# Two transformer blocks in float32: the last column block of the final matmul in three token parts, with accumulating stores

## The chip, the core and the metric

The kernel runs on one core of a Trainium2 chip. A core has five engines that each run their own instructions in order: TensorE (matmuls; PE in the profile, and PEld for its weight loads), VectorE (DVE), ScalarE (ACT), GpSimd (POOL) and SyncE (SP, which here only issues transfers). Transfers can also be issued from ScalarE's and GpSimd's queues. The metric is the time of one execution on the device in microseconds.

## The reference, cut to what matters

Two blocks run one after the other on x, 512 tokens by 1024 channels, in float32. The first holds two gated feed-forward layers and two kinds of attention; the second a convolution, a recurrent mixer and a feed-forward layer with a short convolution. The change touches only the end of the second block:

```python
z = causal_dwconv(h @ w_up, ffn_dw_w, ffn_dw_b)
z_gate, z_val = jnp.split(z, 2, axis=-1)
f = (jax.nn.silu(z_gate) * z_val) @ w_down        # (512, 2816) @ (2816, 1024)
x = x + gt_f * rms_norm(f, ffn_post_g)            # the mean of squares runs over 1024 channels
```

The root mean square of f needs all 1024 channels of a token before any channel of that token can be scaled and added to x.

## The kernel before

Everything is kept transposed: channels lie on the 128 partitions, tokens along the columns, so a tile is 128 channels by 512 tokens and x has eight of them. Each float32 matmul is made of three float32r matmuls (`mm3`, L358): weights and data are split into a high and a low part, and high times high, high times low and low times high are summed in one PSUM bank. The weights come from memory on SyncE's queue, ScalarE rounds the high part and VectorE subtracts to get the low one (`split_weights`, L347). Sums that need no split, such as the mean of squares, are plain fp32 matmuls, which the trace shows as two passes each.

The last stage is `conv_ffn` (L1563). The up matmul gives 22 pairs `hs` of hidden tiles (names hh and hl). Then come eight column blocks m of the down matmul. For m = 0 to 6 a block is 22 × 3 matmuls of 512 tokens (`dense_steps`, L369); its result is squared into `acc` and copied with its gain to `fs[m]` (`done`, L1603). The last block, m = 7, is done in two halves of 256 tokens by `dense_halves` (L420): all 66 matmuls of the first half, then all 66 of the second, from weight tiles that stay in SBUF. `finish(h)` (L1610) sums acc and the last block's squares over the partitions with two matmuls against a constant 1/1024 (`rstd`, L486), forms the reciprocal root in `nrsqrt` (L495; three ScalarE and two VectorE steps), multiplies each of the eight `fs` tiles by it, adds the product to x and stores it in turn through SyncE's and ScalarE's queue. `finish(0)` is issued after the third k of the second half, `finish(1)` after the last matmul.

The program is written in this order, and a scheduler then places the instructions on each engine by their dependences; buffers are taken from pools whose reuse adds waits. Each engine runs its list strictly in that order, so an issue of a transfer that waits holds back all that stands behind it on its engine.

Of the kernel before, what the change touches and what calls it, by code (L numbers as in the profile page):

```python
# [15 lines left out]
ALU = mybir.AluOpType  # L16
# [3 lines left out]
P = 128  # L20
T = 512
D = 1024
KD = D // P
# [2 lines left out]
NH = 8  # L26
BIG = 1.0e30
HALF = slice(0, T // 2), slice(T // 2, T)

# [208 lines left out]
def weave(*streams):  # L240

    total = [sum(c for c, _ in s) or 1.0 for s in streams]
    done, at = [0.0] * len(streams), [0] * len(streams)
    while True:
        left = [i for i, s in enumerate(streams) if at[i] < len(s)]
        if not left:
            return
        i = min(left, key=lambda i: (done[i] + 0.5 * streams[i][at[i]][0]) / total[i])
        cost, f = streams[i][at[i]]
        at[i] += 1  # L250
        done[i] += cost
        f()
# [3 lines left out]
class Net:  # L256
# [160 lines left out]

        return [(1.9, parts), (0.9, sums)]

    def dense_halves(self, src, x, last, done, mid):  # L420

        nk, ws = len(x), []
        for k in range(0, nk, 8):
            n = min(8, nk - k) * P
            part = src[:, k * P : k * P + n]
            ws.append(self.weights(part, n) if k < 16 else self.weights_at(part, n, last))
        for h in range(2):
            ps = self.bank()[:, : T // 2]
            for k in range(nk):
                s = slice(k % 8 * P, k % 8 * P + P)  # L430
                self.mm3(ps, [w[:, s] for w in ws[k // 8]], [t[:, HALF[h]] for t in x[k]], k == 0, k == nk - 1)
                if h == 1:
                    for f in mid.pop(k, ()):
                        f()
            done(h, ps)

    def group_halves(self, src, n, x, room, side, ws=(), done=None, W=6):
# [101 lines left out]
    def swiglu(self, acc, gname, gu, down, new2=None, side=(), start=None):  # L539


        nc = self.nc
        new = self.acc()
        side = list(side)
        with self.phase("h", False) as ph:
            self.log_exp()
            r = self.tmp("r", 1)
            hs = []

            def hidden(pg, pu):  # L550
                m = len(hs)
                s = self.tmp("s")
                nc.vector.tensor_mul(s, pg, r)  # L553
                nc.scalar.activation(s, s, AF.Silu, scale=-1.0)
                self.anchor = nc.vector.tensor_mul(s, s, pu).ins  # L555
                hi = ph.tile([P, T], F32R, tag=f"hh{m}", name=f"hh{m}_{self.n}")
                lo = ph.tile([P, T], F32R, tag=f"hl{m}", name=f"hl{m}_{self.n}")
                self.halves(hi, lo, s)
                hs.append((hi, lo))

            if start is not None:
                self.warm()
                xs = []

                def arrive(k):
                    xs.append(self.first(k))
                    return xs[k]

                ps = self.group(start, 6, arrive)
                self.rstd(self.sq0, self.c("mean"), r)  # L570
                for m in range(3):
                    hidden(ps[2 * m], ps[2 * m + 1])
            else:
                xs = [self.gained(k, self.v(gname, k)) for k in range(KD)]
            for m in range(len(hs), MF):
                pg, pu = self.bank(), self.bank()
                at = gu.shape[0] - 2 * (MF - m)
                self.dense(pg, gu[at], xs)
                if m == 0:
                    self.rstd(acc, self.c("mean"), r)  # L580
                self.dense(pu, gu[at + 1], xs)
                hidden(pg, pu)
                for f in side[:1]:
                    side.pop(0)()
            nc.vector.tensor_scalar_mul(r, r, -0.5)

            def done(m, ps, c=slice(0, T)):
                x = self.x[m][:, c]
                t = self.tmp("s")[:, c]
                nc.vector.tensor_mul(t, ps, r[:, c])  # L590
                self.anchor = nc.vector.tensor_add(x, x, t).ins
                self.add_square(new[:, c], x, m == 0)
                if new2 is not None:
                    self.add_square(new2[:, c], x, m == 0, self.v("fin_g", m))
                    nc.gpsimd.dma_start(self.dY[m][:, c], x)

            if new2 is not None:
                self.entry(new, new2)
            last = KD if new2 is None else KD - 1
            for m in range(last):  # L600
                ps = self.bank()
                n = -(-len(side) // (last - m))
                weave(self.dense_steps(lambda: ps, down[m], hs, split=4), [(1.3, f) for f in side[:n]])
                side = side[n:]
                done(m, ps)
            if new2 is not None:
                enter = [lambda k=k: self.enter(0, k) for k in (None, *range(KD))]
                mid = {4: enter[:1], 5: enter[1:7], 13: enter[7:]}
                tiles = [ph.tile([P, D], F32R, tag="ada", name=f"ada_{self._n()}", bufs=2) for _ in range(2)]
                self.log_exp()  # L610
                self.dense_halves(down[KD - 1], hs, tiles, lambda h, ps: done(KD - 1, ps, HALF[h]), mid)
        return new

    def entry(self, acc1, acc2):
# [948 lines left out]
    def conv_ffn(self, xs, first):  # L1563
        nc, A = self.nc, self.A
        ngt = self.columns(KD)
        nc.vector.scalar_tensor_tensor(ngt, self.mod[:, 40:48], -1.0, self.v("fpost"), op0=ALU.mult, op1=ALU.mult)
        with self.phase("h2", False) as ph:
            tile_ = lambda shape, tag, dt=F32, bufs=1: ph.tile(list(shape), dt, tag=tag, name=f"{tag}_{self._n()}", bufs=bufs)
            hs, zs = {}, {}
# [33 lines left out]
            def done(m, ps, c=slice(0, T)):  # L1603
                if m < KD - 1:
                    self.add_square(acc[:, c], ps, m == 0)
                else:
                    nc.scalar.activation(sq[:, c], ps, AF.Square)
                nc.scalar.activation(fs[m][:, c], ps, AF.Copy, scale=ngt[:, m : m + 1])

            def finish(h):  # L1610
                c = HALF[h]
                self.rstd(acc[:, c], self.c("mean"), r[:, c], last=sq[:, c])
                for k in range(KD):
                    f, x = fs[k][:, c], self.x[k][:, c]
                    nc.vector.tensor_mul(f, f, r[:, c])  # L1615
                    nc.vector.tensor_add(x, x, f)  # L1616
                    (nc.sync if k % 2 == 0 else nc.scalar).dma_start(self.out[k * P : (k + 1) * P, c], x)

            for m in range(KD - 1):
                weave(self.dense_steps(self.bank, A["down2"][m], hs, lambda ps: done(m, ps)))  # L1620
            tiles = [tile_([P, D], f"w{n}", F32R) for n in ("hi", "lo")]
            self.log_exp()
            self.dense_halves(
                A["down2"][KD - 1], hs, tiles, lambda h, ps: done(KD - 1, ps, HALF[h]), {2: [lambda: finish(0)]}
            )
            finish(1)

    def _n(self):
        self.n += 1
# [40 lines left out]
```

## Time and profile before

| | |
|---|---|
| time, median of 3 runs | 1696.13 us (1695.34 to 1698.58) |
| the profiled execution | 1687.92 us, span 1686.1 us |
| TensorE busy | 1649.4 us (98%) |
| its weight loads busy | 1337.2 us (79%) |
| VectorE, ScalarE, GpSimd busy | 1022.9, 716.9 and 51.3 us |
| TensorE's share of the chain that ended last | 89% |
| bytes moved, mean rate | 177.15 MB, 105 GB/s |

A busy TensorE is not one at its peak: matmuls overlap, and a matmul's duration in the profile holds the time that its last column needs to come out. The step from one start to the next is what a stream of them costs. The chain that ended last is followed back from the last instruction; the other engines' time counts only where they are on it.

### The profile page before, as it was taken

To read this page: it belongs to the slowest core of one execution; us is meant where nothing else is said; L and a number is where in the kernel's file an instruction comes from. 1 tells how busy PE (TensorE), PEld (TensorE's weight loads), DVE (VectorE), ACT (ScalarE), POOL (GpSimd) and SP (SyncE) were. 2 spreads that over 40 slices of the span, in tenths; PEclk is the share of its full clock that TensorE was granted. 3 is DMA by queue.
4 is the path that set the end of the run, shared out by engine and by line. 5 is a ranking of instruction groups with operands and counts; after the bars stand their busy time and mean duration, and the time that the engine had idled before them with its cause. 6 is when DMAs were issued, how large, how long until landed. Compare 5 with 4: busy or idle time off the path is not lost.

```text
span 1686.1 us, 21795 instructions
## 1 busy us (share of the span) xinstructions
PE 1649.4 (98%) x8596; PEld 1337.2 (79%) x8596; DVE 1022.9 (61%) x1706; ACT 716.9 (43%) x1167; POOL 51.3 (3%) x104
## 2 busy tenths in 40 slices
PE   9999999999999999999999999998989999999997
PEld 7888888876776788888888887786768988888886
DVE  4555545546888564555334469998777676665224
ACT  4432232237679553223222354633357454444222
POOL 0000000000000000000000010000000000000000
PEclk9999999999999999999999999998999999999999
DMA  5344445534111234443333332221042123333332
GB/s 204 117 146 143 140 126 195 176 100 131 51 62 32 69 90 147 150 149 116 97 100 112 118 114 65 95 71 40 19 141 70 61 87 100 96 92 96 100 95 85
DMA packets 63862, 177.15 MB, mean 105 GB/s; under 512 B 17065, under 2 KB 19369, under 8 KB 63760
## 3 DMA queue, kind: packets, MB, share of 16 engines
q1 hardware_dynamic: 52016, 138.96, 26.5%
q0 software_dynamic: 9872, 34.71, 6.5%
q10 hardware_dynamic: 1872, 2.10, 0.4%
q8 instruction: 67, 1.10, 0.3%
q14 instruction: 35, 0.29, 0.1%
HBM read 169.19 MB, written 6.55 MB: 104 GB/s over the span
## 4 chain that ended last, share of the span: by engine, by line
PE 89%; DVE 6%; ACT 2%; DMA 1%; issue 0%; ACTq 0%; SPq 0%; DVEq 0%
PE ps L321 88%; PE ps L869 1%; DVE Ts L1166 1%; DVE Tm L1163 0%; DMA raw<-in_w_out 0%; DVE acc L484 0%; DVE wlo L351 0%; DVE f L1615 0%; DVE x L1521 0%; DVE x L992 0%; DVE x L1616 0%; DVE x L1522 0%; DMA raw<-in_w_in2k 0%; DMA x<-in_x 0%; DMA dpm<-dY 0%
## 5 line engine op out<-in xcount | busy, mean ns | idle before, releaser
L350 ACT CAST whi<-raw 128x1024 fp32r<-128x1024 f32 (+1 forms) x244 | 249.0, 1021 | 628.1 <-PE ps L321 580.4
L351 DVE TENSOR_TENSOR wlo<-raw,whi 128x1024 fp32r<-128x1024 f32 (+1 forms) x244 | 288.9, 1184 | 256.2 <-ACT whi L350 250.2
L321 PE MATMUL ps<-xh,whi 128*128 128x512 f32 (+1 forms) x1008 | 400.9, 399 | 1.2 <-ACT xh L514 1.2
L321 PE MATMUL ps<-xh,wlo 128*128 128x512 f32 (+1 forms) x1008 | 391.3, 389 | 1.5 <-DVE wlo L351 1.4
L321 PE MATMUL ps<-xl,whi 128*128 128x512 f32 (+1 forms) x1008 | 391.4, 388 | 0.3 <-DVE xl L515 0.3
L321 PEld LDWEIGHTS ps<-xh,whi 128*128 128x128 f32 x1008 | 189.8, 188 | 51.3 <-issue 5.8
L321 PEld LDWEIGHTS ps<-xl,whi 128*128 128x128 f32 x1008 | 189.8, 188 | 44.2 <-issue 5.3
L321 PEld LDWEIGHTS ps<-xh,wlo 128*128 128x128 f32 x1008 | 189.2, 188 | 41.9 <-DVE wlo L351 2.2
L321 PE MATMUL ps<-hh,whi 128*128 128x512 f32 (+1 forms) x560 | 210.5, 376 | 0.0
L321 PE MATMUL ps<-hh,wlo 128*128 128x512 f32 (+1 forms) x560 | 209.8, 375 | 0.0
L321 PE MATMUL ps<-hl,whi 128*128 128x512 f32 (+1 forms) x560 | 209.8, 375 | 0.0
L321 PE MATMUL ps<-oh,whi 128*128 128x512 f32 (+1 forms) x360 | 134.8, 375 | 0.0
L321 PE MATMUL ps<-ol,whi 128*128 128x512 f32 (+1 forms) x360 | 134.5, 374 | 0.0
L321 PE MATMUL ps<-oh,wlo 128*128 128x512 f32 (+1 forms) x360 | 134.2, 373 | 0.0
L321 PEld LDWEIGHTS ps<-hh,whi 128*128 128x128 f32 x560 | 105.4, 188 | 19.9 <-issue 0.8
L321 PEld LDWEIGHTS ps<-hl,whi 128*128 128x128 f32 x560 | 105.4, 188 | 18.9
L321 PEld LDWEIGHTS ps<-hh,wlo 128*128 128x128 f32 x560 | 105.4, 188 | 18.8
L555 DVE TENSOR_TENSOR s<-s,ps 128x512 f32<-128x512 f32 x44 | 30.1, 687 | 133.0 <-PE ps L321 133.0
L321 PEld LDWEIGHTS ps<-ol,whi 128*128 128x128 f32 x360 | 68.2, 189 | 12.2 <-issue 0.2
L321 PEld LDWEIGHTS ps<-oh,whi 128*128 128x128 f32 x360 | 68.0, 189 | 12.0 <-issue 0.2
L321 PEld LDWEIGHTS ps<-oh,wlo 128*128 128x128 f32 x360 | 68.0, 189 | 11.9
L553 DVE TENSOR_TENSOR s<-ps,r 128x512 f32<-128x512 f32 x44 | 30.2, 691 | 73.6 <-PE ps L321 73.5
(444 smaller groups left out, 2173.5 us busy)
## 6 DMA issues: line engine op xcount, KB each, us to landing
raw<-in_ffn_gu SPq DMA_DIRECT2D x82, 512.0 KB, 3.7
ada<-in_ada_w POOLq DMA_DIRECT2D x48, 512.0 KB, 3.9
raw<-in_up SPq DMA_DIRECT2D x38, 512.0 KB, 3.6
raw<-in_ffn_d SPq DMA_DIRECT2D x32, 512.0 KB, 3.7
raw<-in_w_in SPq DMA_DIRECT2D x27, 512.0 KB, 3.6
raw<-in_w_out SPq DMA_DIRECT2D x16, 512.0 KB, 3.6
raw<-in_down SPq DMA_DIRECT2D x16, 512.0 KB, 3.6
raw<-in_ffn_d SPq DMA_DIRECT2D x16, 384.0 KB, 3.2
```

Source lines behind the costliest of these rows:

```text
L321: self.nc.tensor.matmul(*a, **k)
L350: nc.scalar.copy(hi[:, :n], raw[:, :n])
L351: nc.vector.tensor_sub(lo[:, :n], raw[:, :n], hi[:, :n].bitcast(F32))
L553: nc.vector.tensor_mul(s, pg, r)
L555: self.anchor = nc.vector.tensor_mul(s, s, pu).ins
L869: nc.tensor.transpose(ps[:, i * P : (i + 1) * P], es[u, i][:, j * P : (j + 1) * P], self.c("ident"))
L1166: ins = nc.vector.tensor_add(t[:, i + 1 :, :c], t[:, i + 1 :, :c], o)
```

## The change

The last block's 512 tokens are cut in three parts, 256, 128 and 128 (`LAST`); `dense_halves` becomes `dense_parts`, which takes the parts and a table `mid` of work by part and k. The sum for the root is split: `begin(h)` issues the matmul of acc before a part's end (after k = 18 of the same part), `finish(h)` the matmul of the squares, after k = 4 of part 1 for part 0, after k = 6 of part 2 for part 1, and at the end for part 2. The four even x tiles are stored to the output as they are, in the code after m = 3; their products are then added to the output in memory by accumulating transfers from GpSimd. The four odd tiles are added on VectorE as before, into the product's tile, and stored through SyncE and ScalarE. The other user of the function, the first block's end, keeps its two halves.

```diff
--- before.py
+++ after.py
@@ -26,6 +26,7 @@
 NH = 8
 BIG = 1.0e30
 HALF = slice(0, T // 2), slice(T // 2, T)
+LAST = slice(0, T // 2), slice(T // 2, T // 4 * 3), slice(T // 4 * 3, T)
 
 
 
@@ -417,21 +418,20 @@
 
         return [(1.9, parts), (0.9, sums)]
 
-    def dense_halves(self, src, x, last, done, mid):
+    def dense_parts(self, src, x, last, done, mid, parts=HALF):
 
         nk, ws = len(x), []
         for k in range(0, nk, 8):
             n = min(8, nk - k) * P
             part = src[:, k * P : k * P + n]
             ws.append(self.weights(part, n) if k < 16 else self.weights_at(part, n, last))
-        for h in range(2):
-            ps = self.bank()[:, : T // 2]
+        for h, c in enumerate(parts):
+            ps = self.bank()[:, : c.stop - c.start]
             for k in range(nk):
                 s = slice(k % 8 * P, k % 8 * P + P)
-                self.mm3(ps, [w[:, s] for w in ws[k // 8]], [t[:, HALF[h]] for t in x[k]], k == 0, k == nk - 1)
-                if h == 1:
-                    for f in mid.pop(k, ()):
-                        f()
+                self.mm3(ps, [w[:, s] for w in ws[k // 8]], [t[:, c] for t in x[k]], k == 0, k == nk - 1)
+                for f in mid.pop((h, k), ()):
+                    f()
             done(h, ps)
 
     def group_halves(self, src, n, x, room, side, ws=(), done=None, W=6):
@@ -605,10 +605,10 @@
                 done(m, ps)
             if new2 is not None:
                 enter = [lambda k=k: self.enter(0, k) for k in (None, *range(KD))]
-                mid = {4: enter[:1], 5: enter[1:7], 13: enter[7:]}
+                mid = {(1, 4): enter[:1], (1, 5): enter[1:7], (1, 13): enter[7:]}
                 tiles = [ph.tile([P, D], F32R, tag="ada", name=f"ada_{self._n()}", bufs=2) for _ in range(2)]
                 self.log_exp()
-                self.dense_halves(down[KD - 1], hs, tiles, lambda h, ps: done(KD - 1, ps, HALF[h]), mid)
+                self.dense_parts(down[KD - 1], hs, tiles, lambda h, ps: done(KD - 1, ps, HALF[h]), mid)
         return new
 
     def entry(self, acc1, acc2):
@@ -1607,23 +1607,39 @@
                     nc.scalar.activation(sq[:, c], ps, AF.Square)
                 nc.scalar.activation(fs[m][:, c], ps, AF.Copy, scale=ngt[:, m : m + 1])
 
+            def begin(h):
+
+                c = LAST[h]
+                st[h] = ps = self.bank()[:, : c.stop - c.start]
+                self.mm(ps, self.c("mean"), acc[:, c], start=True, stop=False)
+
             def finish(h):
-                c = HALF[h]
-                self.rstd(acc[:, c], self.c("mean"), r[:, c], last=sq[:, c])
-                for k in range(KD):
-                    f, x = fs[k][:, c], self.x[k][:, c]
+
+                c, ps = LAST[h], st[h]
+                self.mm(ps, self.c("mean"), sq[:, c], start=False, stop=True)
+                self.nrsqrt(r[:, c], ps, acc[:, c], 1e-6)
+                for k in (0, 2, 4, 6, 1, 3, 5, 7):
+                    f, o = fs[k][:, c], self.out[k * P : (k + 1) * P, c]
                     nc.vector.tensor_mul(f, f, r[:, c])
-                    nc.vector.tensor_add(x, x, f)
-                    (nc.sync if k % 2 == 0 else nc.scalar).dma_start(self.out[k * P : (k + 1) * P, c], x)
-
+                    if k % 2 == 0:
+                        nc.gpsimd.dma_start(o, f, accum_op=ALU.add)
+                    else:
+                        nc.vector.tensor_add(f, f, self.x[k][:, c])
+                        (nc.sync if k % 4 == 1 else nc.scalar).dma_start(o, f)
+
+            st = {}
             for m in range(KD - 1):
                 weave(self.dense_steps(self.bank, A["down2"][m], hs, lambda ps: done(m, ps)))
+                if m == 3:
+                    for k in range(0, KD, 2):
+                        nc.sync.dma_start(self.out[k * P : (k + 1) * P, :], self.x[k])
             tiles = [tile_([P, D], f"w{n}", F32R) for n in ("hi", "lo")]
             self.log_exp()
-            self.dense_halves(
-                A["down2"][KD - 1], hs, tiles, lambda h, ps: done(KD - 1, ps, HALF[h]), {2: [lambda: finish(0)]}
-            )
-            finish(1)
+            work = lambda f, h: [lambda: f(h)]
+            mid = {(0, 18): work(begin, 0), (1, 4): work(finish, 0), (1, 18): work(begin, 1), (2, 6): work(finish, 1)}
+            mid[2, 18] = work(begin, 2)
+            self.dense_parts(A["down2"][KD - 1], hs, tiles, lambda h, ps: done(KD - 1, ps, LAST[h]), mid, LAST)
+            finish(2)
 
     def _n(self):
         self.n += 1
```

TensorE at the program's end. `ps_…` is the bank that is written, `hh`, `hl` the data, `whi`, `wlo` the weights, `acc` and `sq` the squares, `cst` the constants; the last column is partitions by columns. Before:

```order
L321 MATMUL ps_13197<-hh_1592_12397,whi_13109 128x256
L321 MATMUL ps_13197<-hl_1593_12398,whi_13109 128x256
L321 MATMUL ps_13197<-hh_1592_12397,wlo_13110 128x256
L321 MATMUL ps_13197<-hh_1600_12473,whi_13109 128x256
L321 MATMUL ps_13197<-hl_1601_12474,whi_13109 128x256
L321 MATMUL ps_13197<-hh_1600_12473,wlo_13110 128x256
L321 MATMUL ps_13298<-acc_12477,cst 128x256
L321 MATMUL ps_13298<-sq_12479,cst 128x256
```

After:

```order
L322 MATMUL ps_13384<-acc_12477,cst 128x128
L322 MATMUL ps_13300<-hh_1584_12321,whi_13113 128x128
L322 MATMUL ps_13300<-hl_1585_12322,whi_13113 128x128
L322 MATMUL ps_13300<-hh_1584_12321,wlo_13114 128x128
L322 MATMUL ps_13300<-hh_1592_12397,whi_13113 128x128
L322 MATMUL ps_13300<-hl_1593_12398,whi_13113 128x128
L322 MATMUL ps_13300<-hh_1592_12397,wlo_13114 128x128
L322 MATMUL ps_13300<-hh_1600_12473,whi_13113 128x128
L322 MATMUL ps_13300<-hl_1601_12474,whi_13113 128x128
L322 MATMUL ps_13300<-hh_1600_12473,wlo_13114 128x128
L322 MATMUL ps_13384<-sq_12479,cst 128x128
```

The acc sum now stands ahead of the last nine matmuls, not behind them, and the matmuls have 128 columns. Each of the two new parts has 66 of them.

ScalarE from the first part's Ln to the last part's square. `sq` and `f_1612` read the last block's bank; `r` and `acc` are the reciprocal root's steps; a DMA row is a store that waits for VectorE. Before:

```order
L499 ACTIVATE r_12478<-ps_13207,eps 128x256
L500 ACTIVATE r_12478<-r_12478 128x256
L501 ACTIVATE acc_12477<-r_12478 128x256
L1617 DMA out<-x_1323_10027 128x256
L1617 DMA out<-x_1335_10099 128x256
L1617 DMA out<-x_1347_10171 128x256
L1607 ACTIVATE sq_12479<-ps_13197 128x256
L1608 ACTIVATE f_1612_12487<-ps_13197,col_10986 128x256
L1617 DMA out<-x_1356_10240 128x256
L499 ACTIVATE r_12478<-ps_13298,eps 128x256
```

After:

```order
L501 ACTIVATE acc_12477<-r_12478 128x256
L1628 DMA out<-f_1608_12483 128x256
L1628 DMA out<-f_1612_12487 128x256
L1607 ACTIVATE sq_12479<-ps_13203 128x128
L1608 ACTIVATE f_1612_12487<-ps_13203,col_10986 128x128
L499 ACTIVATE r_12478<-ps_13287,eps 128x128
L500 ACTIVATE r_12478<-r_12478 128x128
L501 ACTIVATE acc_12477<-r_12478 128x128
L1628 DMA out<-f_1608_12483 128x128
L1628 DMA out<-f_1612_12487 128x128
L1607 ACTIVATE sq_12479<-ps_13300 128x128
```

A part's square stands behind two stores of the part before it, where three stood ahead of the second half's square and one ahead of its Ln.

SyncE at the start of the up matmul (`raw` from `in_up` are weight loads; `out` is the result). Before:

```order
L349 DMA raw_11006<-in_up 128x1024
L349 DMA raw_11056<-in_up 128x1024
L349 DMA raw_11110<-in_up 128x1024
L349 DMA raw_11146<-in_up 128x1024
L349 DMA raw_11186<-in_up 128x1024
L349 DMA raw_11222<-in_up 128x1024
```

After:

```order
L350 DMA raw_11006<-in_up 128x1024
L350 DMA raw_11056<-in_up 128x1024
L1635 DMA out<-x_1320_10010 128x512
L1635 DMA out<-x_1329_10063 128x512
L1635 DMA out<-x_1341_10135 128x512
L1635 DMA out<-x_1352_10206 128x512
L350 DMA raw_11110<-in_up 128x1024
L350 DMA raw_11146<-in_up 128x1024
L350 DMA raw_11186<-in_up 128x1024
L350 DMA raw_11222<-in_up 128x1024
```

The stores of x, four transfers of 128 × 512, went ahead of the third load of the up weights, which is long before the down stage. On GpSimd's queue the twelve accumulating transfers (four of 256, eight of 128 tokens) stand at the very end.

## Rows read from the trace of the kernel before

**Rows 1.** The page: shares by engine of the chain that ended last.

```profile
PE 89%; DVE 6%; ACT 2%; DMA 1%; issue 0%; ACTq 0%; SPq 0%; DVEq 0%
```

**Rows 2.** Timeline, TensorE, the last block's two halves (start us, duration us, engine, instruction).

```profile
1664.67 0.28 PE L321 MATMUL ps<-hh,wlo 128*128 128x256 f32 x1
...
1665.87 0.60 PE L321 MATMUL ps<-acc,cst 128*128 128x256 f32 x2
1666.30 0.59 PE L321 MATMUL ps<-sq,cst 128*128 128x256 f32 x2
...
1666.85 0.28 PE L321 MATMUL ps<-hl,whi 128*128 128x256 f32 x1
...
1673.45 0.28 PE L321 MATMUL ps<-hh,wlo 128*128 128x256 f32 x1
...
1674.28 0.70 PE L321 MATMUL ps<-sq,cst 128*128 128x256 f32 x2
```

**Rows 3.** Timeline, TensorE, a whole column block; 90 steps lie between the two.

```profile
1630.13 0.39 PE L321 MATMUL ps<-hh,wlo 128*128 128x512 f32 x1
...
1650.53 0.39 PE L321 MATMUL ps<-hh,wlo 128*128 128x512 f32 x1
```

**Rows 4.** Timeline, TensorE and its weight loads, three groups of eight fp32 passes.

```profile
375.16 1.05 PE L321 MATMUL ps<-cst,acc 128*128 128x1 f32 x8
...
375.16 0.97 PEld L321 LDWEIGHTS ps<-cst,acc 128*128 128x128 f32 x8 [0.44 <-DVE acc L484]
...
1171.26 2.07 PE L321 MATMUL ps<-vt,kbt 128*128 128x128 f32 x8 [0.67 <-ACT vt L1386]
...
1206.64 1.16 PE L321 MATMUL ps<-vt,kbt 128*128 128x128 f32 x8
```

**Rows 5.** Timeline, ScalarE and its queue, last block.

```profile
1657.80 0.59 ACT L483 ACTIVATE sq<-ps 128x512 f32<-128x512 f32 x1
...
1664.99 0.38 ACT L1607 ACTIVATE sq<-ps 128x256 f32<-128x256 f32 x1 [3.87 <-PE ps L321]
...
1666.93 0.47 ACT L499 ACTIVATE r<-ps,eps 128x256 f32<-128x256 f32 x1 [1.20 <-PE ps L321]
...
1673.85 0.38 ACT L1607 ACTIVATE sq<-ps 128x256 f32<-128x256 f32 x1 [5.54 <-DVE f L1615]
...
1675.19 0.47 ACT L499 ACTIVATE r<-ps,eps 128x256 f32<-128x256 f32 x1 [0.60 <-PE ps L321]
...
1683.06 0.34 ACTq L1617 DMA_DIRECT2D out<-x  x1
```

**Rows 6.** Timeline, VectorE: the mixer's end, a 512-column step, the last half.

```profile
1321.12 0.42 DVE L1522 TENSOR_TENSOR x<-x,Ts 128x256 f32<-128x256 f32 x1
...
1644.12 0.69 DVE L484 TENSOR_TENSOR acc<-acc,sq 128x512 f32<-128x512 f32 x1
...
1677.57 0.76 DVE L1615 TENSOR_TENSOR f<-f,r 128x256 f32<-128x256 f32 x2
...
1682.27 0.75 DVE L1616 TENSOR_TENSOR x<-x,f 128x256 f32<-128x256 f32 x2
```

**Rows 7.** Transfers by tile and queue: count, KB each, us from issue to landing.

```profile
out<-x ACTq DMA_DIRECT2D x8, 128.0 KB, 1.7
...
dY<-x POOLq DMA_DIRECT2D x2, 128.0 KB, 3.0
...
vec<-in_vec POOLq DMA_DIRECT2D x1, 238.0 KB, 6.9
```

**Rows 8.** Line 595, stores from GpSimd: its time for one, min/median/max in ns.

```profile
L595 POOL DMA_DIRECT2D dY<-x x9: 539/539/549, 875.6 to 986.3; - x9
```

**Rows 9.** Timeline, SyncE's queue, second and third load of the up weights.

```profile
1315.56 0.33 SPq L349 DMA_DIRECT2D raw<-in_up  x1
...
1337.27 0.33 SPq L349 DMA_DIRECT2D raw<-in_up  x1
```

**Rows 10.** Busy time by engine in a stretch; after POOL, the granted clock (1.00 is full).

```profile
1171.20:1173.30 2.10, 2.04 (x10) 1.82 (x10) 0.00 (x0) 0.01 (x1) 0.00 (x0) 0.50 0.20 31
```

## The prediction

> **What bounds the kernel now.** I read the shares of the chain that ended last first: TensorE holds 89% of it, VectorE 6% [rows 1]. So a microsecond of TensorE time is a microsecond of the kernel, and the other engines count where they are the chain. Then the timeline of the last stretch, engine by engine, because the change lies there. The last output column block (m = 7) runs as two halves of 256 tokens, 66 matmuls each: 22 blocks of k by three terms. Neighbouring starts lie 0.120 us apart: (1673.45 − 1666.85) / 55 [rows 2]. Whole blocks of 512 tokens run at (1650.53 − 1630.13) / 90 = 0.227 us [rows 3]. After the last matmul (start 1673.45) TensorE has only the sum of squares left, and a serial tail follows: square on ScalarE, sum on TensorE, Ln, Exp and Square on ScalarE, two VectorE steps, then from 1677.57 sixteen VectorE operations of 256 columns [rows 5, 6], the last stores, and the end at 1686.1. I cut the tail at that first VectorE multiply, f0: 4.12 us from the last matmul's start to f0, 8.53 us from f0 to the end.
>
> **The matmuls of the last block.** Removed: 66 of 256 columns, 66 × 0.120 = 7.92 us. Added: 132 of 128 columns, each with its own load of 128 × 128 weights, for a new part loads all its weights again. No row of before shows a matmul with float32r operands and fewer than 256 columns, so its step has to be bounded. The nearest row is the one with almost no columns: eight fp32 passes with one moving column and 128 × 128 weights take (1.05 − 0.25) / 7 = 0.114 us each, where 0.25 is the duration of one, and their weight loads (0.97 − 0.19) / 7 = 0.111 us [rows 4]. With nothing to stream, that is the weight load. Eight fp32 passes with 128 columns at the full clock step by (1.16 − 0.27) / 7 = 0.127 us [rows 4]; fp32 streams a column slower than float32r, so this lies above. The 256-column step of 0.120 hides a load wholly and is the other end for a stream without a stall. I take 0.114, the row without columns, and keep 0.111 and 0.120. Added: 132 × 0.114 = 15.05 us, net +7.13 (14.65 and 15.84 at the ends, +6.7 and +7.9).
>
> The Trainium skill (TensorE: Matmul & The Clock Gate, section "LDWEIGHTS (loading the stationary operand)") puts a load at its columns divided by 1.2, 107 ns for 128; the trace has 111 to 114. By the page the term would be 132 × 0.107 − 7.92 = +6.2 us.
>
> **The sums of squares.** Four fp32 passes of 256 columns (two of acc, two of sq) cost 1666.85 − 1665.87 less one matmul, 0.98 − 0.12 = 0.86 us; they stay in the path, acc now in part 0. New in the path, ahead of the last matmul: acc and sq of part 1 and acc of part 2, six passes of 128 columns at 0.111 to 0.127 [rows 4], 0.7 us. TensorE's last matmul so starts 7.13 + 0.7 = 7.8 us later.
>
> **From the last matmul to f0.** The first half shows this path undisturbed: last matmul 1664.67 to square 1664.99, 0.32 us; in the second half it takes 0.40, and Ln starts at 1675.19, 0.91 after the sum began at 1674.28, where the first half needs 1666.93 − 1666.30 = 0.63 [rows 2, 5]: ScalarE first issues a store that waits for VectorE. With 128 columns and a free ScalarE: 0.32 − 0.05 = 0.27; the square 0.28 (0.59 at 512, 0.38 at 256 columns [rows 5]); 0.05 to the sum; the sum 0.42 (0.63 less two passes of some 0.107); from Ln to f0 now 2.38 (1675.19 to 1677.57), less 3 × 0.105 on ScalarE and 2 × 0.135 on VectorE, where 512 and 256 columns differ by (0.69 − 0.42) us [rows 6], gives 1.80. Sum 2.82 against 4.12: −1.3 us.
>
> **From f0 to the end.** Now: 16 operations at (1682.27 − 1677.57) / 14 = 0.336 us, the last store issued at 1683.06, landing 1.7 us later (1684.8), then 1.34 us to the end [rows 5 to 7]. After: 12 operations of 128 columns at 0.336 − 0.133 = 0.203, the last over at 11 × 0.203 + 0.29 = 2.5 us after f0; its store lands at 4.3, the end is at 5.6. The four accumulating transfers take the other path. Their multiplies come first, so GpSimd starts at f0 + 0.33 and needs 0.54 us for each [rows 8]: the fourth starts at 1.94. An accumulating transfer is not in the trace. The last plain stores land in 1.7 us, GpSimd's two stores of 128 KB in 3.0, the slowest transfer of its queue in 6.9 [rows 7]. I take 3.0, the store nearest in size: 1.94 + 3.0 + 1.34 = 6.3 us against 8.53, −2.25 us. Ends: at 1.7 the store through ScalarE is last and the tail is 5.6 (−2.9); at 6.9 it is 10.2 (+1.65).
>
> By the Trainium skill (DMA: Bandwidth & Descriptors, section "Anatomy of one DMA — SWDGE (gpsimd) path") a transfer costs about 2.0 us plus its bytes over 436 GB/s, 2.15 us for 64 KB. By that the fourth would land before the ScalarE store, and this term would be −2.9.
>
> **Costed at nothing.** The four stores of x (256 KB each) stand on SyncE's queue behind the second load of the up weights, as the order shows, not in the down stage. They wait for the last x of the mixer (1321.12 + 0.42 [rows 6]); SyncE has issued that load by 1315.9 and its next goes out at 1337.27 [rows 9], so 15 us of idle queue hide four issues and 1 MB. Without that gap each issue would cost 0.33 us of a load's lead. On GpSimd's queue nothing stands behind the twelve accumulating transfers, as the order shows. ScalarE's queue is in order: the square of part 1 stands behind two stores that wait for VectorE's part 0. From the start of part 1, with a step of 0.114: f0 of part 0 at 4.7, last add 8.8, store 9.2, square done 9.5; its sum stands after the 21st matmul of part 2, at 10.6, 1.1 us of cover. ScalarE is free again at 15.7, 0.6 us before it is wanted for part 2 at 16.3.
>
> **Sum.** +7.8 − 1.3 − 2.25 = +4.3 us on the profiled 1687.92 us, 1692.2. The three timed runs have a median of 1696.13, 8 us above the profiled execution; I add the same to the median: 1700.4. With the ends of the step and the faster landing, 3.2 to 5.1, so 1699.3 to 1701.2.
>
> **Rivals.**
> Loads hide better (not slower): if a 128-column step is half of the 256-column one, 0.060, the extra matmuls cost nothing. For it: 256-column steps carry a load in 0.120 without showing it. Against it: a load with nothing else to do steps by 0.111 [rows 4]. But then ScalarE's order decides: part 1 ends at 4.6 us, its square waits behind the stores until about 8.4, TensorE stands before the sum, and ScalarE comes free for part 2 only at 13.8. f0 at 13.8 + 2.55 = 16.4, end at 22.7, against 1686.1 − (1664.67 + 0.12) = 21.3 now, and 0.4 for the sum moved into part 0: +1.8 us, 1697.9. It decides below a step of about 0.09. The same skill page (section "Back-to-back issue gap") gives some 81 ns for a matmul of 128 columns with its load in a stream; at 0.081 the same walk ends at +2.2 us, 1698.3.
> Steps twice as long: float32r at 128 columns costs as much as 512 (0.227), or the clock falls to 1.2 GHz, where the 128-column passes at a granted 0.50 step by (2.07 − 0.27) / 7 = 0.257 [rows 4, 10]. For it: the low clock appears where TensorE had waited before; against: nothing here waits, the stream is whole. 132 × 0.227 − 7.92 + 0.7 − 3.55 = +19 us, 1715.
> Slow accumulation: the transfer reads, adds and writes; at 6.9 us to landing +7.8 − 1.3 + 1.65 = +8.2, 1704.3.
>
> **How the numbers follow.** Forecast 0.68, better-hidden loads 0.10, double step 0.10, slow accumulation 0.12. About 0.2%, 3.4 us, is what a measurement can tell from no change. Of the forecast's 0.68 I give 0.17 to landing inside it (3.2 to 3.4 and the spread of the runs), 0.01 to ending faster; of the better-hidden loads 0.07 is no change, 0.03 faster. So slower 0.72, same 0.24, faster 0.04. The range leaves out the double step and the odd ends: 1696.5 to 1706; the forecast's own is 1699 to 1702.5.
>
> **What the profile will show.** Right: steps of 0.111 to 0.120 us in 132 matmuls, weight loads back to back and TensorE's last matmul 7.4 to 8.6 us later; f0 2.8 us behind it; 12 operations in 2.5 us; the last landing from GpSimd's queue. Wrong: steps under 0.09, or a TensorE wait ahead of the sum of part 1; a granted clock near 0.5 in parts 1 and 2; accumulating transfers that land within 1.7 us or beyond 5; a late load of the up weights.

## The result, and the profile after

The changed kernel takes 1706.89 us (median of six runs, 1701.66 to 1711.68), the kernel before 1696.27 (six runs, 1692.46 to 1698.58): a ratio of 1.0072, with an interval of 1.0051 to 1.0092, or 10.6 us more. The forecast was 1700.4 us, 4.3 us more: the right direction, less than half of the size, and the time lies above the upper end of the stated range, 1706.

The two profiled executions can't be subtracted whole (1687.92 and 1709.36 us): one lies below all six timed runs of its kernel, the other above its median. What lies ahead of the last column block is the same work but for four stores of x, and yet its first matmul starts at 1656.87 us in one and at 1667.27 in the other. The experiments show that this is not the change: two kernels whose code is that of before up to the last block, without a store of x, start it at 1658.14 and at 1672.17. (The mean granted clock differs with it: 0.989 and 0.979 in the first two, 0.987 and 0.980 in these.) So everything below is counted in one stretch, from the first matmul of the last column block (m = 7) to the end of the span. It is 29.23 us before and 40.23 after, a difference of 11.0, and that agrees with the 10.6 of the medians.

| stretch, us | before | after | difference | forecast |
|---|---|---|---|---|
| first matmul of the block to the start of the last | 16.58 | 24.01 | +7.43 | +7.8 |
| last matmul's start to f0, the last part's first VectorE multiply | 4.12 | 2.96 | −1.16 | −1.3 |
| f0 to the end | 8.53 | 13.26 | **+4.73** | **−2.25** |
| sum | 29.23 | 40.23 | +11.00 | +4.3 |

TensorE's timeline in the last block of the changed kernel, to be read beside [rows 2] (start us, duration us, engine, instruction):

```profile
1667.27 0.28 PE L322 MATMUL ps<-hh,whi 128*128 128x256 f32 x1
...
1677.77 0.28 PE L322 MATMUL ps<-hl,whi 128*128 128x128 f32 x1
...
1682.23 0.27 PE L322 MATMUL ps<-hh,wlo 128*128 128x128 f32 x1
...
1691.28 0.27 PE L322 MATMUL ps<-hh,wlo 128*128 128x128 f32 x1
1691.92 0.49 PE L322 MATMUL ps<-sq,cst 128*128 128x128 f32 x2 [0.37 <-ACT sq L1607]
```

Forty 128-column steps lie between the second row and the third: 4.46 / 40 = 0.1115 us each, the low end of the forecast (0.111). The busy time by stretch, one row for each part, says that the clock was full throughout and that TensorE never stood. After the stretch and its length come busy us (and instructions) of PE, PEld, DVE, ACT and POOL, then the granted clock, the busy share of the DMA engines and GB/s:

```profile
1667.27:1675.60 8.33, 8.33 (x70) 8.28 (x68) 2.79 (x3) 4.21 (x5) 0.00 (x0) 1.00 0.08 31
1675.60:1683.46 7.86, 7.86 (x71) 7.81 (x70) 4.08 (x12) 2.06 (x5) 2.17 (x4) 1.00 0.10 8
1683.46:1691.40 7.94, 7.94 (x73) 7.94 (x72) 4.10 (x17) 1.52 (x5) 3.99 (x6) 1.00 0.85 153
```

The tail, on the other engines, against [rows 5, 6]:

```profile
1691.59 0.28 ACT L1607 ACTIVATE sq<-ps 128x128 f32<-128x128 f32 x1 [4.15 <-PE ps L322]
...
1692.44 0.37 ACT L499 ACTIVATE r<-ps,eps 128x128 f32<-128x128 f32 x1 [0.32 <-PE ps L322]
...
1694.24 1.30 DVE L1623 TENSOR_TENSOR f<-f,r 128x128 f32<-128x128 f32 x6
1694.83 3.49 POOL L1625 DMA_DIRECT2D out<-f  x4 [2.59 <-DVE f L1623]
...
1696.27 0.49 DVE L1627 TENSOR_TENSOR f<-f,x 128x128 f32<-128x128 f32 x2
```

VectorE is done at 1696.76, 2.5 us after f0, as forecast. GpSimd needs 3.49 us for four issues, 0.87 each where the plain stores of [rows 8] need 0.54. Then no engine does anything until 1707.5. The transfers are not what is waited for. The DMA activity from 1692 to 1707.6 in 40 slices of 0.39 us (tenths of the 16 engines busy) ends in the 20th slice, at 1699.8:

```profile
DMA  9999000000399969998800000000000000000000
```

Nor does SyncE wait for them any longer: at the kernel's closing line (L1675) it waits 3.1 us for the last landing and then 6.2 us for the other engines. (The row names TensorE's sequencer, which was long done. The wait ends near 1706.9, just after the GpSimd record shown next.) Its waits, and the closing records of the other engines at that line (for each: shortest, median and longest in ns, then the first start and the last):

```profile
SPq L1675 <- PEq L1675: 6.7, 2, 6.2
SPq L1675 <- DMA out<-f: 3.1, 1, 3.1
```

```profile
L1675 POOLq DRAIN  x3: 46/98/10429, 1696.3 to 1707.2; - x3
...
L1675 PEldq DRAIN  x2: 13/276/538, 1691.9 to 1707.0; - x2
L1675 DVEq DRAIN  x2: 19/214/409, 1696.4 to 1707.0; - x2
L1675 ACTq DRAIN  x2: 8/79/150, 1697.2 to 1707.0; - x2
```

There it is: a closing **drain on GpSimd** of 10.43 us, from 1696.3 to 1706.7. (The record opens before the last issue has ended, so it is longer than what follows the issue.) It ends 8.4 us after GpSimd's last issue (1694.83 + 3.49 = 1698.32), and 0.8 us later the span is over. No other engine's drain lasts over 0.54 us. The kernel before has the same record:

```profile
L1659 POOLq DRAIN  x3: 93/179/8084, 1255.4 to 1685.7; - x3
```

It took 8.08 us there too, but at 1255.4, behind GpSimd's last transfers in the mixer and beside 420 us of other work. The chain of waits of before therefore never showed it, and the prediction never looked at the closing records.

Of the edits costed at nothing, the stores of x held. SyncE's queue in the changed kernel:

```profile
1326.89 5.37 SPq L1635 DMA_DIRECT2D out<-x  x4
1347.64 2.50 SPq L350 DMA_DIRECT2D raw<-in_up  x2
```

The four are issued by 1332.3, and the next load of the up weights goes out 15 us later; the queue was idle there before, too [rows 9].

### The profile page after: what moved, and what is told of

The parts are those of the page before. It is cut to its first block, busy times and chain, and to the rows that moved or that the text cites. A ratio compares the mean times of both kernels' runs of the same rounds, so it can differ in the third digit from the quotient of the medians.

```text
span 1707.5 us, 21971 instructions
## 1 busy us (share of the span) xinstructions
PE 1667.9 (98%) x8666; PEld 1353.7 (79%) x8666; DVE 1021.8 (60%) x1712; ACT 718.1 (42%) x1172; POOL 61.9 (4%) x116
## 4 chain that ended last, share of the span: by engine, by line
PE 90%; DVE 5%; ACT 2%; DMA 2%; issue 0%; POOL 0%; POOLq 0%; ACTq 0%; DVEq 0%
PE ps L322 88%; PE ps L869 1%; DMA raw<-in_ffn_k 1%; DVE wlo L352 1%; DVE Ts L1166 1%; DVE Tm L1163 0%; DVE acc L484 0%; PE ps L1326 0%; DVE x L1521 0%; DMA raw<-in_w_in2k 0%; DVE x L1522 0%; DMA raw<-in_w_out 0%; DMA dpm<-dY 0%; DVE xl L515 0%; ACT whi L351 0%
## 5 line engine op out<-in xcount | busy, mean ns | idle before, releaser
L322 PE MATMUL ps<-hh,whi 128*128 128x512 f32 (+2 forms) x582 | 216.5, 372 | 0.0
L322 PE MATMUL ps<-hh,wlo 128*128 128x512 f32 (+2 forms) x582 | 215.7, 371 | 0.0
L322 PE MATMUL ps<-hl,whi 128*128 128x512 f32 (+2 forms) x582 | 215.6, 371 | 0.0
L322 PEld LDWEIGHTS ps<-hh,whi 128*128 128x128 f32 x582 | 109.6, 188 | 19.9 <-issue 0.8
L322 PEld LDWEIGHTS ps<-hl,whi 128*128 128x128 f32 x582 | 109.7, 188 | 19.0
L322 PEld LDWEIGHTS ps<-hh,wlo 128*128 128x128 f32 x582 | 109.6, 188 | 18.8
```

The source lines that it names most:

```text
L322: self.nc.tensor.matmul(*a, **k)
```

## The experiments

Theory A: the end waits for GpSimd's closing drain, which ends some 8 us after GpSimd's last issue, whatever else goes on. Theory B: the accumulating transfers land late, since they read, add and write, and the end waits for them. Theory C: the three parts are the whole cost. The runs of one kernel spread by 5 us and more to either side, so beside each ratio to the kernel before (with its interval) stands the stretch from the last block's first matmul to the end, in us.

| kernel | stretch | ratio to before |
|---|---|---|
| before | 29.23 | 1 |
| changed | 40.23 | 1.0072 (1.0051 to 1.0092) |
| three parts alone | 34.18 | 1.0021 (1.0001 to 1.0040) |
| changed, plain stores from GpSimd | 38.83 | 1.0053 (1.0028 to 1.0079) |
| changed, accumulation in the first two parts alone | 33.87 | 1.0025 (1.0006 to 1.0044) |
| before, last store from GpSimd | 35.72 | 1.0039 (1.0018 to 1.0061) |
| before, first half stored from GpSimd | 28.63 | 0.9993 (0.9968 to 1.0018) |
| accumulation alone, in halves | 33.72 | 1.0020 (0.9998 to 1.0043) |
| before, first half stored from SyncE alone | 29.06 | 0.9981 (0.9960 to 1.0001) |
| the same, two tiles computed on GpSimd | 32.29 | 1.0028 (1.0009 to 1.0047) |
| before, one column copied on GpSimd at the end | 35.03 | 1.0035 (1.0014 to 1.0056) |
| parts of 288 and 224 | 28.50 | 0.9979 (0.9958 to 0.9999) |

### Three parts alone

```diff
-                for k in (0, 2, 4, 6, 1, 3, 5, 7):
+                for k in range(KD):
                     nc.vector.tensor_mul(f, f, r[:, c])
-                    if k % 2 == 0:
-                        nc.gpsimd.dma_start(o, f, accum_op=ALU.add)
-                    else: ...
+                    nc.vector.tensor_add(f, f, self.x[k][:, c])
+                    (nc.sync if k % 2 == 0 else nc.scalar).dma_start(o, f)
...
```

The four early stores of x are gone too.

> Three parts, but no accumulating transfer and no early store of x: all eight tiles are added on VectorE and stored through SyncE and ScalarE. Measured from the first matmul of the last column block to the end of the span (29.23 us before, 40.23 after). Theory A (GpSimd's closing drain, a record of 10.4 us at the end of the changed kernel, is what the end waits for): last matmul 24.0 us into the block as in the changed kernel, f0 3.0 later, sixteen VectorE operations of 128 columns 3.35 us, 3.1 us from the last add to the end: 33.4 us, 6.8 less than the changed kernel, 4.2 more than before, so about 1700.5 us. Theory B (the accumulating transfers land late, and the end waits for them): the same 33.4 us, as it too loses them. Theory C (the three parts are the cost and the transfers are innocent): 38 to 40 us, 1705 to 1707.

Measured: 34.18 us, 6.05 less than the changed kernel. C falls; A and B stand. The sixteen operations of 128 columns and plain stores take 6.24 us from f0 to the end against 8.53 before, so the narrow last part alone gives back 2.3 us, as much as the prediction had expected of the whole change there. The 0.8 us over the expected 33.4 come from ScalarE's queue:

```profile
1678.25 3.02 ACTq L1625 DMA_DIRECT2D out<-f  x3
1681.32 0.28 ACT L1607 ACTIVATE sq<-ps 128x128 f32<-128x128 f32 x1 [6.88 <-PE ps L322]
...
1684.90 2.76 ACTq L1625 DMA_DIRECT2D out<-f  x4
1687.71 0.28 ACT L1607 ACTIVATE sq<-ps 128x128 f32<-128x128 f32 x1 [4.48 <-PE ps L322]
```

The rows are ScalarE and its queue. Both squares start only when stores that wait for VectorE have been issued. The first makes TensorE stand 0.41 us ahead of part 1's sum, and its last matmul starts 0.64 us later in the block than in the changed kernel. The second comes 0.64 us after the last matmul's start (1687.07), in the changed kernel 0.31. That is 1.0 us in all; from f0 on the run took 0.2 less than expected.

### The changed kernel with plain stores from GpSimd

```diff
-                        nc.gpsimd.dma_start(o, f, accum_op=ALU.add)
+                        nc.gpsimd.dma_start(o, f)
```

> The changed kernel, with the twelve accumulating transfers as plain stores from GpSimd's queue; the four even tiles then lack x in the output. Counted from the last block's first matmul. Theory A (closing drain of GpSimd, 7.4 to 8.4 us after its last issue has ended, whatever the transfer does; then 0.8 us to the end): four issues of 0.54 instead of 0.87 us move the last issue's end forward by 1.3 us, so 38 to 39 us against 40.2, and the drain's record stays near 10 us. Theory B (read, add and write make the landing late): a plain store lands in 3.0 us, so f0 (27.0) + 1.94 + 3.0 + 1.34 = 33.3 us, 7 us less than the changed kernel.

Measured: 38.83 us, in A's 38 to 39 and far from B's 33.3. GpSimd's last issues, the drain, and SyncE's wait:

```profile
1687.12 2.13 POOL L1625 DMA_DIRECT2D out<-f  x4 [3.92 <-DVE f L1623]
```

```profile
L1675 POOLq DRAIN  x3: 46/97/9031, 1688.6 to 1698.2; - x3
```

```profile
SPq L1675 <- PEq L1675: 6.9, 2, 6.4
```

Without the accumulation the issues are 0.53 us each and the drain still ends 8.4 us after the last of them (1697.6 − 1689.25). B falls as the cause of the end. What accumulation adds is 1.4 us of the 40.2, by its slower issue.

### Accumulation in the first two parts alone

```diff
-                    if k % 2 == 0:
+                    if k % 2 == 0 and h < 2:
                         nc.gpsimd.dma_start(o, f, accum_op=ALU.add)
...
```

The lines left out spread the last part's eight stores over SyncE and ScalarE and end the early stores of x at token 384.

> The changed kernel, with accumulating transfers in the first two parts only; the last part of 128 tokens is added on VectorE and stored through SyncE and ScalarE, and the early stores of x cover only the first 384 tokens. Theory A (closing drain): GpSimd's last issue ends 25.0 us into the block, its drain 7.4 to 8.4 us later, the end 0.8 after that: 33.2 to 34.2 us, beside 33.4 by way of VectorE and the last stores; so 33.4 to 34.2, 6 to 7 us less than the changed kernel. Theory B (late landing): the accumulating transfers of part 1 land before the last part's stores, 33.4 us, and no long drain at the end.

Measured: 33.87 us, within the 33.2 to 34.2. GpSimd's last issue and its drain:

```profile
1682.73 3.49 POOL L1625 DMA_DIRECT2D out<-f  x4 [3.95 <-DVE f L1623]
```

```profile
L1675 POOLq DRAIN  x3: 46/98/10107, 1684.2 to 1694.8; - x3
```

The drain ends at 1694.3, 8.1 us after the last issue, and the span at 1695.1. Though the last part's stores go through SyncE and ScalarE, the drain of the part before still ends last: f0 to the end is 6.90 us against the 6.24 of the run without accumulation.

### The kernel before, with one store from GpSimd

```diff
-  (nc.sync if k % 2 == 0 else nc.scalar).dma_start(...)
+  (nc.gpsimd if h == 1 and k == KD - 1 else nc.sync if k % 2 == 0 else nc.scalar).dma_start(...)
```

> The kernel before, with one edit: the very last store (tile 7, second half, 128 KB, plain) goes through GpSimd's queue instead of ScalarE's. Theory A (closing drain): the last add ends 26.2 us into the block, the issue takes 0.54, the drain ends 7.4 to 8.4 later and the span 0.8 after: 34.9 to 35.9 us against 29.2 in the kernel before, 5.7 to 6.7 us slower, about 1702 to 1703. Theory B (accumulation lands late, a plain store does not): issue 0.54 for 0.33 and landing 3.0 for 1.7 us, 1.5 us slower, about 1698.

Measured: 35.72 us, A's 34.9 to 35.9, and 1.0039 by the medians. One plain store of 128 KB, which lands in 2.0 us, is enough. The drain ends at 1704.1, 7.5 us after the issue's end, and the span 1.2 us later:

```profile
1696.02 0.54 POOL L1617 DMA_DIRECT2D out<-x  x1 [429.92 <-DVE x L1616]
```

```profile
L1659 POOLq DRAIN  x3: 46/232/8069, 1696.0 to 1705.0; - x3
```

### The control: GpSimd's stores in the first half

```diff
-  (nc.sync if k % 2 == 0 else nc.scalar).dma_start(...)
+  (nc.gpsimd if h == 0 else nc.sync if k % 2 == 0 else nc.scalar).dma_start(...)
```

> The kernel before, with the eight plain stores of the first half (128 KB each) on GpSimd's queue; the second half is stored through SyncE and ScalarE as before. A control for the closing drain. Theory A (the drain ends 7.4 to 8.4 us after GpSimd's last issue has ended, and costs only what sticks out): the last add of the first half ends 16.6 us into the last column block, its issue 0.5 later, the drain at 24.5 to 25.5, before the last landing at 27.9: no change in the tail, 28.9 to 29.3 us from the block's first matmul to the end against 29.2, and a drain record of about 8 us that ends before the last stores land. Theory D (GpSimd's transfers at the end of the program cost by themselves, by their number, or by making VectorE slower): 8 transfers cost more than the one of the fourth experiment, over 35 us.

Measured: no slower (0.9993), and 28.63 us, 0.3 under A's 28.9 to 29.3. The last issues and the drain:

```profile
1690.03 1.07 POOL L1617 DMA_DIRECT2D out<-x  x2 [0.27 <-DVE x L1616]
```

```profile
L1659 POOLq DRAIN  x3: 46/98/8656, 1690.5 to 1700.5; - x3
```

It lasts 8.66 us and ends at 1699.2, 1.6 us before the span does. Eight transfers that are issued early cost nothing where one issued last costs 6.5 us. So it is the time of the last issue that counts, and not the number. The margin is small: the last store lands at 1699.85, 0.7 us after the drain's end. Of the 0.6 us under the kernel before, 0.25 is ScalarE's queue (below). The rest lies behind that landing: some 0.9 us to the end, against 1.34 before. Why the closing steps are shorter there stays open.

### Accumulation alone, in halves

```diff
-                for k in range(KD): ...
+                for k in (0, 2, 4, 6, 1, 3, 5, 7):
+                    nc.vector.tensor_mul(f, f, r[:, c])
+                    if k % 2 == 0:
+                        nc.gpsimd.dma_start(o, f, accum_op=ALU.add)
+                    else: ...
...
```

The odd tiles and the four early stores of x are as in the changed kernel.

> The other half of the change alone: two parts of 256 tokens as before, but x of the four even tiles stored early and their sum made by accumulating transfers, in both halves; no part of 128 tokens. Theory A: f0 20.7 us into the block as before, multiplies of 0.336, GpSimd from 21.1, four issues of 0.87: the last issue's end at 24.6 to 24.9, drain 8.4 later at 33.0 to 33.3, the end 0.8 after: 33.8 to 34.1 us, 4.6 to 4.9 more than before, about 1698 us. Theory C (the cost of the change is in the three parts alone): 12 VectorE operations in place of 16, so the tail shortens by 1.3 to 2 us, 27.2 to 28 us.

Measured: 33.72 us, beside A's 33.8 to 34.1 and far from C's 27 to 28 (the medians alone, 0.9998 to 1.0043, would not settle it). From f0 on the trace has:

```profile
1684.23 2.10 DVE L1615 TENSOR_TENSOR f<-f,r 128x256 f32<-128x256 f32 x6
1684.95 3.49 POOL L1617 DMA_DIRECT2D out<-f  x4 [4.30 <-DVE f L1615]
```

f0 to the end is 1697.4 − 1684.23 = 13.17 us with 256 columns, where the changed kernel has 13.26 with 128. With GpSimd last, the tail is the start of its four issues, the issues, the drain and 0.8 us, and together these come to the same within 0.1 us at either width. That is why the two halves of the change cost more together (11.0) than one by one (5.0 + 4.5): the 2.3 us that the narrow part gives back alone are no longer on the path. The difference is smaller, 1.6 us, because the changed kernel is spared most of what ScalarE's queue costs the parts alone.

The same trace has the price of the transfers themselves (count, KB each, median us from issue to landing):

```profile
out<-f POOLq DMA_DIRECT2D x8, 128.0 KB, 4.8
out<-f SPq DMA_DIRECT2D x4, 128.0 KB, 4.0
out<-f ACTq DMA_DIRECT2D x4, 128.0 KB, 4.0
```

In the control the eight plain stores from GpSimd land in 2.0 us, and those of SyncE and ScalarE in 1.7. Beside accumulating transfers these plain ones too need 4.0 us.

### All stores of the first half on SyncE's queue

```diff
-  (nc.sync if k % 2 == 0 else nc.scalar).dma_start(...)
+  (nc.sync if k % 2 == 0 or h == 0 else nc.scalar).dma_start(...)
```

> The kernel before, with all stores of the first half on SyncE's queue, so that no store that waits for VectorE stands ahead of ScalarE's square and Ln of the second half. By the trace of before, the square starts 0.40 us after the last matmul's start against 0.32 in the first half, and Ln 0.91 after the sum against 0.63. If ScalarE's order makes that difference: 0.36 us less, 28.9 us from the last block's first matmul to the end against 29.2. Rival: the difference comes from TensorE running empty (no matmul behind the sum) and not from ScalarE's queue: no change, 29.2.

Measured: 29.06 us. The last matmul's start to f0 is 3.87 us instead of 4.12, so ScalarE's order made 0.25 of the expected 0.36; from f0 to the end it is 8.61 (8.53 before). The ratio, 0.9981 (0.9960 to 1.0001), can't be told from no change.

### Two tiles computed on GpSimd

```diff
-                for k in range(KD):
+                for k in (0, 1, 3, 4, 5, 7, 2, 6):
+                    e = nc.gpsimd if h == 1 and k in (2, 6) else nc.vector
-                    nc.vector.tensor_mul(f, f, r[:, c])
-                    nc.vector.tensor_add(x, x, f)
+                    e.tensor_mul(f, f, r[:, c])
+                    e.tensor_add(x, x, f)
...
```

The lines left out order the stores over SyncE and ScalarE.

> As the run before this one, and in the second half two of the eight tiles are multiplied and added on GpSimd instead of VectorE; GpSimd issues no transfer, its tiles are stored through SyncE and ScalarE, last in their queues. Two questions. Does work that is no transfer lengthen GpSimd's closing drain? Theory A (only transfers do): the drain record stays at about 8 us right after the last transfer near 1260 us and the end is free of it. Rival (any late work on GpSimd does): a drain of about 8 us after the last add, 34 to 37 us. And the time: VectorE has 12 operations of 0.336 us, 4.0 instead of 5.4; if GpSimd does an operation within 1.0 us and does not slow VectorE, 27.5 to 27.9 us from the block's first matmul to the end against 29.2; at 1.5 us an operation 29.5 to 30.

Measured: 32.29 us, slower than before (1.0028). Theory A as it stood, a drain after transfers only, falls here, and the rival's drain ends the run. Its 34 to 37 us came out too long, since GpSimd is done 24.0 us into the block and VectorE only at 26.7. GpSimd issues no transfer, and still:

```profile
1681.55 1.29 DVE L1616 TENSOR_TENSOR f<-f,r 128x256 f32<-128x256 f32 x2
1681.74 1.68 POOL L1616 TENSOR_TENSOR f<-f,r 128x256 f32<-128x256 f32 x2 [422.64 <-DVE r L503]
1682.76 1.80 DVE L1617 TENSOR_TENSOR x<-x,f 128x256 f32<-128x256 f32 x2
1683.38 1.76 POOL L1617 TENSOR_TENSOR x<-x,f 128x256 f32<-128x256 f32 x2
```

```profile
L1662 POOLq DRAIN  x3: 46/93/9117, 1683.5 to 1693.1; - x3
```

Its last operation ends at 1685.14, the drain at 1692.6, 7.5 us later, and the span at 1693.4. The operations themselves took 0.84 to 0.88 us, within the 1.0 that was hoped for. Against [rows 6] VectorE's pairs of operations rise from 0.75 us to between 1.27 and 1.80 us while GpSimd works and are back at 0.74 when it is done, so its last operation ends 6.2 us after f0 instead of the 4.0 of twelve operations. The Trainium skill (SBUF — State Buffer, section "Who interferes with whom") says that a VectorE instruction with two inputs in SBUF contends with a GpSimd instruction that reads SBUF; the trace agrees.

### One column on GpSimd

```diff
                     (nc.sync if k % 2 == 0 else nc.scalar).dma_start(...)
+                if h == 1:
+                    nc.gpsimd.tensor_copy(sq[:, :1], x[:, :1])
```

> The kernel before, with one GpSimd instruction added at the very end: a copy of one column (128 x 1) of the last finished tile into a tile that nobody reads any more. No transfer on GpSimd's queue, no work taken from VectorE; all stores as before. Theory A as it stood (only GpSimd's transfers are followed by a long closing drain): no change, 29.2 us from the last block's first matmul to the end. Theory A2 (after the run with two tiles computed on GpSimd, whose drain ended 7.5 us after its last operation: the drain follows GpSimd's last instruction of any kind): the copy ends 0.1 to 0.3 us after the last add at 26.2, the drain 7.4 to 7.5 later, the end 0.8 after: 34.5 to 34.8 us, 5.3 to 5.6 more than before, about 1699 us.

Measured: 35.03 us and 1.0035. One instruction of 0.19 us, with no transfer and nothing waiting for its result, costs 5.8 us:

```profile
L1619 POOL COPY sq<-x x1: 187/187/187, 1693.2 to 1693.2; 128x1 f32<-128x1 f32 x1
```

```profile
L1661 POOLq DRAIN  x3: 46/97/7635, 1693.1 to 1701.3; - x3
```

The drain ends at 1700.7, 7.4 us after the copy. Theory A2 holds: GpSimd's closing drain follows its last instruction of any kind.

### Parts of 288 and 224

```diff
+LAST = slice(0, 288), slice(288, T)
-            ... lambda h, ps: done(KD - 1, ps, HALF[h]), {2: [lambda: finish(0)]}
+            ... lambda h, ps: done(KD - 1, ps, LAST[h]), {2: [lambda: finish(0)]}, LAST
```

with all stores of the first part on SyncE.

> A version meant to be faster than both kernels: two parts of 288 and 224 tokens instead of 256 and 256, and the first part's stores all on SyncE's queue; no GpSimd. By the steps measured (0.227 us for 512 columns, 0.120 for 256, 0.1115 for 128, the weight load): 66 x (0.1275 + 0.1115) = 15.8 us of matmuls against 15.84; the last matmul to f0 0.25 us shorter by ScalarE's queue as in the run before and 0.25 by 32 columns fewer in its seven steps; sixteen VectorE operations of 0.303 instead of 0.336, 0.5 us less: 28.2 us from the last block's first matmul to the end against 29.2 before. Rival (a width that is no multiple of 128 or 256 runs slower): 66 steps of 0.227 in either part, 30 us of matmuls, 43 us.

Measured: 28.50 us against the expected 28.2, and a ratio of 0.9979 (0.9958 to 0.9999). It is the fastest version here, if only by about what a measurement can tell.

```profile
1667.40 0.29 PE L322 MATMUL ps<-hh,whi 128*128 128x288 f32 x1
...
1676.08 0.26 PE L322 MATMUL ps<-hh,whi 128*128 128x224 f32 x1
...
1684.30 0.28 PE L322 MATMUL ps<-hh,wlo 128*128 128x224 f32 x1
```

66 steps of 288 columns take 8.68 us, 0.1315 each (0.1275 expected), which makes the 0.3 us over the expected time. Steps of 224 columns lie 0.112 us apart, as those of 128 do (0.1115), and a load with next to no columns takes 0.111 [rows 4]: between 128 and 224 columns the weight load sets the step, and more columns cost nothing.

## Why the prediction was wrong

**The matmuls and the sums of squares** (+7.13 and +0.7, so +7.8): measured +7.43. The step was 0.1115 where 0.114 was taken, and the row of loads alone, 0.111 in [rows 4], was the better neighbour. The rivals of a hidden load and of a double step fell with it, and the clock stayed at 1.00.

**From the last matmul to f0** (−1.3): measured −1.16. ScalarE came free ahead of part 2 as worked out: its two stores went out by 1691.07, the square at 1691.59.

**From f0 to the end** (−2.25): measured +4.73. This is the step that failed, by 7.0 us. The prediction ended this path at the last landing plus 1.34 us, and among what it costed at nothing stands: "On GpSimd's queue nothing stands behind the twelve accumulating transfers". GpSimd's closing drain does. Two of its sizes were off. An issue was taken at 0.54 us and is 0.87; the landing was taken at 3.0 us and is 3.6 for 64 KB. Together they are small: SyncE's wait for the last landing ends at some 1697.0 + 3.1 = 1700.1, and with the 1.34 us to the end that the prediction used the tail would have been 7.2 us instead of 6.3. The other 6.1 us are a term that the sum did not have. In the kernel before the tail does end behind the last landing, since GpSimd is done long before. The change makes GpSimd the last engine at work, and brings its closing drain from 1255 us, where it was free, to the end: it ends 8.4 us after the last issue, and the span 0.8 us later.

**The rival of a slow accumulation** (1704.3) came nearest to the time, for the wrong reason: the transfers do land later than plain ones, but with plain stores in their place the drain still ends the kernel (38.83 us). The prediction's own test, landings beyond 5 us, would not have found the cause: the medians are 4.6 and 3.6, the longest is 5.5.

**The stores of x, and ScalarE's cover:** right. The square of part 1 started behind its two stores at 1684.83, its sum at 1685.92 without a wait.

What stays open is what GpSimd does in the drain. Its end lies 7.4 to 7.5 us after the last instruction where that is a copy, an operation or a single store, and 8.1 to 8.4 after groups of stores; no run here tells why.

## What to carry to other kernels

Before work goes to an engine that has been idle for long at the end, read the closing records of every engine in the trace, and not only the chain that ended last: a fixed cost that lies under other work today comes to light when that engine becomes the last. In this kernel GpSimd must be done some 9 us before the end (7.4 to 8.4 us of drain and 0.8 behind it). In the control its eight stores, done by then, cost nothing; one column copied at the very end cost 5.8 us. And where weight loads set the step of a matmul, cut a block into parts no narrower than the load hides: here a step of 128 columns took as long as one of 224.

## What the runs showed of the hardware

The closing drain of GpSimd is the surprise: 7.6 to 10.4 us by its record in every kernel of this study, against at most 0.75 us on the other engines in the traces of before and after. The Trainium skill (VectorE: DVE Perf Modes, section "The DRAIN you can't avoid") puts the runtime's own drains, ahead of a kernel and behind it, at some 12 ns on all five engines. Whether the record at this program's closing line is one of those, no run here shows; GpSimd's is of another size.

Accumulating transfers load the DMA engines: in the last row of the stretches above their share is 0.85 while 153 GB/s move. With plain stores from GpSimd in their place the same stretch has 0.47 at 151 GB/s, and in the last half of the kernel before 0.37 goes with 125 GB/s:

```profile
1673.50:1686.10 12.60, 1.36 (x6) 0.56 (x5) 7.64 (x22) 2.05 (x5) 0.00 (x0) 0.74 0.37 125
```
